# A gate projection moved from the attention heads into the product groups of the gate stage, with the first output projection as filler in its place

## The chip, the cores and the metric

The kernel runs on one core of a Trainium2 chip. The metric is the device time of one execution in microseconds (us); smaller is better. The engines named below are PE (TensorE, the matrix engine), DVE (VectorE), ACT (ScalarE), POOL (GpSimd) and SP (SyncE, which here only issues DMAs).

## The reference

One decoder block with two attention branches that read the same normalised input h (512 tokens, width 1024):

```python
proj = h @ w_in[layer]
fq, fk, fv, fz, mq, mk, mv, mz, ga, gb, fl = split_cols(proj, IN_SPLITS)
...
y_fox = from_heads(fox_attention(q, k, v, log_f)) * jax.nn.silu(fz)
...
y_moba = from_heads(moba_attention(q, k, v)) * jax.nn.silu(mz)
merged = (jax.nn.sigmoid(ga + b_gate[layer, 0]) * (y_fox @ w_fox[layer])
          + jax.nn.sigmoid(gb + b_gate[layer, 1]) * (y_moba @ w_moba[layer]))
x = x + merged @ w_out[layer]
```

Both branches have 8 heads of 64 columns, so q, k, v and z are 512 columns wide each; ga and gb have 1024 columns each. With 512 tokens the second branch sees at most its own block of 256 keys and the one before it, which together are all earlier keys: both branches are causal attention over 512 keys.

## The kernel before

**Numbers in two parts.** Every float32 operand of a large product is split into a high part in the matrix engine's reduced format and a low part, the rest. A product is then three matmuls (high by high, high by low, low by high). A split costs one ACT copy (`wh_...`, line 140) and one DVE subtraction (`wl_...`, line 142) for each 128x1024 block of weights. At most four split blocks exist at a time (tags `wh` and `wl`), and four raw blocks (`wr`), which SP loads in order as their buffers come free.

**Stages.** First come q and k of the first half of the first branch. Then follow the 16 heads, in four groups of four: first branch halves a and b (`f a`, `f b`), second branch halves a and b (`m a`, `m b`). After them stand the gates (`GA0`, `GA1` for ga, `GB0`, `GB1` for gb), the merge with the second output projection (`wm0` to `wm3`), and w_out.

**A head.** `Aa(h)` makes four tiles of logits (`lg`, 128, 256, 384 and 512 columns, two PSUM buffers); DVE takes the row maximum of each (line 574), ACT the exponential (576). `Bb(h)` transposes the tiles on PE (`p_a`, `p_b`, `p_cc`, three PSUM buffers of tag `tp`), ACT and DVE split them (`pth` 621, `ptl` 622), and PE multiplies by v (`pv`, 625 and 626; v is the stationary operand, tiles `v_mva`, `v_mvb`, tag `v`, two buffers). ACT and DVE then copy and add the two halves (`ysh` 650, `ypair` 651). `Tr` transposes q and k of a pair of heads (`p_qT`, `p_kT`, also tag `tp`), followed by ACT copies (538, 541, 543) and DVE remainders (539, 546). `sums_out` and `sums_in` send the inverse row sums through DRAM (`p_ri`, then the DMAs of lines 599 and 605, both on ACT's queue). `Yp` multiplies y by the inverse sums and by z (POOL 665, DVE 666) and splits it (667, 668).

**Fillers.** Between the steps of the heads stand units of projections that keep PE occupied: a list for each group of four heads, in `plan`. A q, k or v unit is 24 matmuls of 256 columns, a z unit (`unit_z`) 24 of 512 columns, a unit of the first output projection w_fox (`unit_f`, names wf0 to wf3, two units each) 12 of 512 columns. Filler results lie in two PSUM buffers (tag `pj`) until they are copied out; `unit_f` of wf0 copies into `f03`, a tile of tag `v`. The order in the program text is only the first order: the framework's scheduler then orders the instructions of all engines by its own estimates, and each engine works through its own list strictly in order.

**Groups of seven products.** Each of GA0, GA1, GB0 and GB1 makes two blocks of 256 columns by 512 tokens as seven products of half size in place of eight, in the manner of Strassen and Winograd: four on sums of the input halves (`S1` to `S4`, made in the first group of heads, kept in DRAM and loaded into SBUF by POOL's DMAs in `load_sums`) and three on the input itself (`A11`, `A12`, `A22`). One product is 24 matmuls of 256 columns. Four raw weight blocks (11, 12, 22, 21, loaded in this order) give seven weight operands (`prep`, with four subtractions on line 718). `PRODUCTS` sets the order of the products and `evac` what is kept or added after each.

## Time and profile before

| what | us |
|---|---|
| median of three runs | 424.02 |
| lowest and highest of them | 423.7, 426.01 |
| span of the profiled execution | 421.9 |
| PE busy in it | 416.7 |
| DVE busy | 326.8 |
| ACT busy | 280.4 |
| POOL busy | 101.7 |

The span runs from the first to the last instruction of the profiled execution; the 2.1 us between it and the median lie around it. PE is busy in 99% of the span, and the chain that ended last is 97% PE. So the kernel is read as a row of matmuls with hardly a hole, in which the other engines have to be on time. In the trace a matmul's duration overlaps that of its successor, so the price of one in a row is the distance between starts.

### The profile page before, as it was taken

The numbers are of one execution on the slowest core, as the hardware profiler recorded it, in microseconds if no ns is written. First come the engines' busy times: TensorE is split into PE (matmuls) and PEld (weight loads), VectorE is DVE, ScalarE is ACT, GpSimd is POOL, SyncE is SP. The second block draws the span as 40 slices with busy tenths as digits, with TensorE's granted clock in tenths as the row PEclk, the third lists the DMA queues.
The fourth block names the chain that finished last, engine by engine and source line by source line (L and its number), as shares of the span: only waits on it lengthen the run. The fifth ranks groups of instructions, "written<-read, shape, count | busy, mean of one in ns | idle before, by whom it ended". The sixth has DMA issues, their size and how long they took to land.

```text
span 421.9 us, 7677 instructions
## 1 busy us (share of the span) xinstructions
PE 416.7 (99%) x2909; PEld 387.6 (92%) x2909; DVE 326.8 (77%) x574; ACT 280.4 (66%) x529; POOL 101.7 (24%) x119
## 2 busy tenths in 40 slices
PE   8999999999999999999999999999999999999996
PEld 6998899999999998899998888899999989988885
DVE  4669968799968778568666779767979698689883
ACT  5987327877867978569758687655756535686450
POOL 1067600223236550015650101211000000022230
PEclk9999999999999999999999999999999999999999
DMA  7982335567153123303122310674052603697484
GB/s 237 391 285 99 99 101 162 154 195 223 59 172 103 42 87 101 97 29 99 36 92 76 101 50 27 233 248 143 26 177 64 236 2 112 220 248 119 100 136 164
DMA packets 24660, 56.37 MB, mean 134 GB/s; under 512 B 2864, under 2 KB 7664, under 8 KB 24624
## 3 DMA queue, kind: packets, MB, share of 16 engines
q1 hardware_dynamic: 13536, 38.11, 27.7%
q0 software_dynamic: 3392, 8.39, 8.8%
q10 hardware_dynamic: 7696, 9.38, 7.0%
q8 instruction: 23, 0.38, 0.4%
q14 instruction: 13, 0.11, 0.1%
HBM read 48.37 MB, written 6.32 MB: 130 GB/s over the span
## 4 chain that ended last, share of the span: by engine, by line
PE 97%; DMA 1%; SPq 0%; DVE 0%; issue 0%
PE pb_GB L757 3%; PE pb_GA L757 3%; PE pb_GB L754 3%; PE pb_GA L756 3%; PE pb_GB L756 3%; PE pb_GA L754 3%; PE po L945 3%; PE po L944 3%; PE po L943 3%; PE pv L626 2%; PE lg L572 2%; PE pv L625 2%; PE lg L571 2%; PE pf L684 2%; PE pf L683 2%; PE pf L685 2%
## 5 line engine op out<-in xcount | busy, mean ns | idle before, releaser
L342 POOL TENSOR_TENSOR ff<-ss,mh 128x8 f32<-128x8 f32 x16 | 29.7, 1861 | 73.2 <-DVE ss L340 67.4
L576 ACT ACTIVATE p<-p,negm 128x128 f32<-128x128 f32 (+1 forms) x64 | 35.7, 559 | 11.7 <-DVE negm L574 10.6
L574 DVE CUSTOM_DVE_ANT_0 p<-lg,mask 128x128 f32<-128x128 f32 (+1 forms) x64 | 30.8, 487 | 14.4 <-PE lg L572 13.9
L892 POOL DMA_DIRECT2D wr_o<-in_w_out_dram x4 | 4.9, 1279 | 89.3 <-DMA wr_o<-in_w_out_dram 81.1
L140 ACT ACTIVATE wh_GB<-wr_gb 128x1024 fp32r<-128x1024 f32 x14 | 14.6, 1059 | 10.1 <-PE pm L684 3.5
L571 PE MATMUL lg<-KH,QS 128*128 128x128 f32 (+1 forms) x64 | 20.4, 328 | 0.0
L906 DVE TENSOR_TENSOR wl_o<-wr_o,wh_o 128x1024 fp32r<-128x1024 f32 x14 | 17.0, 1222 | 3.8 <-ACT wh_o L905 3.8
L142 DVE TENSOR_TENSOR wl_GB<-wr_gb,wh_GB 128x1024 fp32r<-128x1024 f32 x14 | 16.9, 1223 | 3.9 <-ACT wh_GB L140 3.9
L905 ACT ACTIVATE wh_o<-wr_o 128x1024 fp32r<-128x1024 f32 x14 | 14.9, 1061 | 7.5 <-PE pb_GB L756 2.8
L142 DVE TENSOR_TENSOR wl_GA<-wr_ga,wh_GA 128x1024 fp32r<-128x1024 f32 x14 | 16.9, 1222 | 2.8 <-ACT wh_GA L140 2.3
L140 ACT ACTIVATE wh_GA<-wr_ga 128x1024 fp32r<-128x1024 f32 x14 | 14.6, 1057 | 5.9 <-PE pb_GA L756 2.7
L651 DVE TENSOR_TENSOR ypair<-pv,ysh 64x512 f32<-64x512 f32 x16 | 11.0, 687 | 6.6 <-ACT ysh L650 6.4
L622 DVE TENSOR_TENSOR ptl<-p_a,pth 128x512 fp32r<-128x512 f32 x16 | 11.0, 685 | 4.9 <-ACT pth L621 4.8
L650 ACT ACTIVATE ysh<-pv 64x512 f32<-64x512 f32 x16 | 9.5, 594 | 7.9 <-PE pv L626 5.5
L546 DVE SCALAR_TENSOR_TENSOR KL<-p_kT,cs,KH 64x512 fp32r<-64x512 f32 x16 | 12.0, 748 | 3.3 <-ACT KH L543 3.0
L336 DVE TENSOR_REDUCE ss<-sq 128x8 f32<-128x512 f32 x16 | 10.8, 680 | 4.3 <-ACT sq L335 4.2
L756 PE MATMUL pb_GA<-Gl,wh_GA 128*128 128x256 f32 x48 | 13.7, 285 | 0.0
L757 PE MATMUL pb_GA<-Gh,wl_GA 128*128 128x256 f32 x48 | 13.5, 281 | 0.0
L754 PE MATMUL pb_GA<-Gh,wh_GA 128*128 128x256 f32 x48 | 13.5, 280 | 0.0
L757 PE MATMUL pb_GB<-Gh,wl_GB 128*128 128x256 f32 x48 | 13.5, 281 | 0.0
L756 PE MATMUL pb_GB<-Gl,wh_GB 128*128 128x256 f32 x48 | 13.4, 281 | 0.0
L754 PE MATMUL pb_GB<-Gh,wh_GB 128*128 128x256 f32 x48 | 13.3, 281 | 0.0
(456 smaller groups left out, 1792.0 us busy)
## 6 DMA issues: line engine op xcount, KB each, us to landing
wr_ga<-in_w_in_dram SPq DMA_DIRECT2D x8, 512.0 KB
wr_gb<-in_w_in_dram SPq DMA_DIRECT2D x8, 512.0 KB
wr_o<-in_w_out_dram SPq DMA_DIRECT2D x8, 512.0 KB
xt<-in_xT_dram SPq DMA_DIRECT2D x8, 256.0 KB
x<-in_x_dram SPq DMA_DIRECT2D x8, 256.0 KB
s_dramh<-sum_sh ACTq DMA_DIRECT2D x8, 256.0 KB
s_draml<-sum_sl ACTq DMA_DIRECT2D x8, 256.0 KB
rinv_bc<-r_dram ACTq DMA_DIRECT2D x16, 128.0 KB
```

What stands on the lines that cost most here:

```text
L140: A.activation(hi[:, :, 0:n], src, AF.Copy)
L142: eng.tensor_tensor(out=lo[:, q, 0:n], in0=src[:, q], in1=hi[:, q, 0:n].bitcast(F32), op=OP.subtract)
L342: G.tensor_tensor(out=f2, in0=ss.rearrange("p t h -> p (t h)"), in1=mh, op=OP.pow)
L571: T.matmul(lg[:, :n], qs[:, qt], kh[:, :n], start=True, stop=False)
L574: V.tensor_tensor_reduce(pt, lg[:, :n], mask[:, 512 - n:512], -0.125, 3.0e38, op0=OP.add, op1=OP.min, accum_out=mkn[:, hh, i:i + 1])
L576: A.activation(pt, pt, AF.Exp, bias=mkn[:, hh, i:i + 1], scale=-1.0, accum_out=rs[:, hh, i:i + 1])
L754: T.matmul(o, hi[:, k, cc], lh, start=(n < 3 and c == 0 and k == 0), stop=False, skip_group_check=True)
L756: T.matmul(o, hi[:, k, cc], ll, start=False, stop=False, skip_group_check=True)
L757: T.matmul(o, lo[:, k, cc], lh, start=False, stop=(k == 3), skip_group_check=True)
L905: A.activation(wide(hi), wide(R[key, c]), AF.Copy)
L906: V.tensor_tensor(out=wide(lo), in0=wide(R[key, c]), in1=wide(hi).bitcast(F32), op=OP.subtract)
L943: T.matmul(o, gh, hi[:, c, r, :], start=(new and k == 0), stop=False, skip_group_check=True)
```

## The change

The second branch's z (mz, names mza and mzb) is no longer projected by four `unit_z` among the heads. It becomes a group of seven products like the gates, `GZ0`, ahead of GA0. Its results go through tanh and z in `finish_z`, and y of the second branch (kept as `YM`, without z) is multiplied by z there and split (`y_parts`). The filler lists move up: mqb goes to the group `f b`, the group `m a` has mkb and mvb, and the group `m b` has wf0 to wf3. The two wf3 units that stood behind the last head are gone from there. In all groups A12 changes place with S3, so the second product needs the raw block 21 and no sums.

```diff
--- before.py
+++ after.py
@@ -507,7 +507,15 @@
                 G.memset(tl[rows, :].bitcast(F32), 0.0)
 
 
-    Y = {}
+    Y, YM = {}, {}
+
+    def y_parts(br, gp, y):
+        yh = t2("y", 15, f"yh{br}{gp}", dt=F32R)
+        yl = t2("y", 15, f"yl{br}{gp}", dt=F32R)
+        A.activation(yh, y, AF.Copy)
+        V.tensor_tensor(out=yl, in0=y, in1=yh.bitcast(F32), op=OP.subtract)
+        Y[br, gp] = (yh, yl)
+
     mkn = con.tile([P, 16, 4], F32, name="negm")
     rs = con.tile([P, 16, 4], F32, name="rsum")
     ri = con.tile([P, 16, 4], F32, name="rinv")
@@ -659,14 +667,14 @@
             def go():
                 y = st["y", pr]
                 gp = 2 * (half == "b") + pr
-                yh = t2("y", 15, f"yh{br}{gp}", dt=F32R)
-                yl = t2("y", 15, f"yl{br}{gp}", dt=F32R)
                 zr = st["r", pr]
+                if not fox:
+                    ym = YM[gp] = t2("y", 15, f"ym{gp}")
+                    V.tensor_tensor(out=ym, in0=y, in1=zr, op=OP.mult)
+                    return
                 G.tensor_tensor(out=zr, in0=ZS[br, gp], in1=zr, op=OP.mult)
                 V.tensor_tensor(out=y, in0=y, in1=zr, op=OP.mult)
-                A.activation(yh, y, AF.Copy)
-                V.tensor_tensor(out=yl, in0=y, in1=yh.bitcast(F32), op=OP.subtract)
-                Y[br, gp] = (yh, yl)
+                y_parts(br, gp, y)
             return go
 
 
@@ -704,12 +712,12 @@
 
 
 
-    PRODUCTS = (("A11", 1), ("S3", 3), ("A12", 2), ("S2", 1), ("S1", 1), ("A22", 3), ("S4", 1))
+    PRODUCTS = (("A11", 1), ("A12", 2), ("S3", 3), ("S2", 1), ("S1", 1), ("A22", 3), ("S4", 1))
     groups = {}
 
     def group(name):
-        ga, i = name[1] == "A", int(name[2])
-        wa, wb = (f"g{'a' if ga else 'b'}{i}", f"g{'a' if ga else 'b'}{i + 2}")
+        ga, gz, i = name[1] == "A", name[1] == "Z", int(name[2])
+        wa, wb = ("mza", "mzb") if gz else (f"g{'a' if ga else 'b'}{i}", f"g{'a' if ga else 'b'}{i + 2}")
         st = {}
         R, B = {}, {}
         base = len(preps)
@@ -726,14 +734,14 @@
         def prep(n):
 
             def go():
-                if n == 1:
+                if n == 2:
                     sub(R["11"], R["12"], R["11"])
                     sub(R["12"], R["22"], R["12"])
                 elif n == 3:
                     sub(R["12"], R["22"], R["11"])
                 elif n == 5:
                     sub(R["21"], R["21"], R["12"])
-                key = ("11", "12", "21", "12", "11", "21", "22")[n]
+                key = ("11", "21", "12", "12", "11", "21", "22")[n]
                 B[n] = split(R[key], CW, f"{name}{n}")
             return go
         for key, nm, hf, last in (("11", wa, 0, 4), ("12", wb, 0, 5), ("22", wb, 1, 6), ("21", wa, 1, 5)):
@@ -775,9 +783,9 @@
                     u = [v4[:, 0:2, :], v4[:, 2:4, :]]
                 st["u"] = u
                 keep(1, 1)
+            elif n == 2:
+                keep(3, 3)
             elif n == 1:
-                keep(3, 3)
-            elif n == 2:
                 add(st["u"][0], 0, 1, 2)
             elif n == 3:
                 keep(2, 1)
@@ -789,7 +797,21 @@
             else:
                 finish(1)
 
+        def finish_z(q):
+            u = st["u"][q]
+            for c in range(2):
+                s = t2("u", 4, "sg")
+                for h in ((slice(0, S),) if q == 0 else (slice(0, HT), slice(HT, S))):
+                    z = two(st[1])[:, c, :] if q and h.start == 0 else u[:, c, h]
+                    A.activation(s[:, h], z, AF.Tanh, scale=0.5)
+                    V.scalar_tensor_tensor(u[:, c, h], s[:, h], 1.0, z, op0=OP.add, op1=OP.mult)
+                ym = YM[2 * q + c]
+                G.tensor_tensor(out=ym, in0=u[:, c, :], in1=ym, op=OP.mult)
+                y_parts("m", 2 * q + c, ym)
+
         def finish(q):
+            if gz:
+                return finish_z(q)
             u, j0 = st["u"][q], 2 * i + 4 * q
             bg = C_BG + (0 if ga else 8)
             for c in range(2):
@@ -989,8 +1011,8 @@
         groups["WO"] = late_loads
 
 
-    order = ["fqa", "fka", "fza", "fzb", "fva", "fqb", "fkb", "fvb", "mqa", "mka", "mva", "mza", "mqb", "mkb", "mvb", "mzb", "wf0", "wf1", "wf2", "wf3",
-             "GA0", "GA1", "GB0", "wm0", "wm2",
+    order = ["fqa", "fka", "fza", "fzb", "fva", "fqb", "fkb", "fvb", "mqa", "mka", "mva", "mqb", "mkb", "mvb", "wf0", "wf1", "wf2", "wf3",
+             "GZ0", "GA0", "GA1", "GB0", "wm0", "wm2",
              "GB1", "wm1", "wm3", "WO"]
     for nm in order[2:]:
         stream(nm)
@@ -1059,9 +1081,9 @@
     zero_kl()
     rope_tables()
     plan = (("f", "a", C_FQ, C_FK, ["fqb", "fkb", "fvb", "mqa"]),
-            ("f", "b", C_FQ, C_FK, ["mka", "mva", "mza"]),
-            ("m", "a", C_MQ, C_MK, ["mqb", "mkb", "mvb"]),
-            ("m", "b", C_MQ, C_MK, ["mzb", "wf0", "wf1", "wf2"]))
+            ("f", "b", C_FQ, C_FK, ["mka", "mva", "mqb"]),
+            ("m", "a", C_MQ, C_MK, ["mkb", "mvb"]),
+            ("m", "b", C_MQ, C_MK, ["wf0", "wf1", "wf2", "wf3"]))
     head, body, tail, gate = attn_group("f", "a", col(C_FQ), col(C_FK))
     head[0]()
     for n in range(4):
@@ -1094,10 +1116,9 @@
             at = 2
             body, tail = nxt[1][:at] + gate + nxt[1][at:], nxt[2]
             gate = nxt[3]
-    seq(["wf3"])
     enter("gates")
     load_sums()
-    fill = filler(["GA0", "GA1", "GB0"])
+    fill = filler(["GZ0", "GA0", "GA1", "GB0"])
     for n, u in enumerate(fill):
         u()
         if n == 2:
```

On PE, where the first units of wf0 stand among the last heads of `m a`, the kernel before has (pz_mzb is the second z unit of mzb, pf_3376 the first unit of wf0):

```order
L413 MATMUL pz_mzb_3329<-Gh,wh_mzb_3017 128x512
L571 MATMUL lg<-KH,QS 128x128
L572 MATMUL lg<-KL_852,QS 128x128
L414 MATMUL pz_mzb_3329<-Gl,wh_mzb_3017 128x512
L415 MATMUL pz_mzb_3329<-Gh,wl_mzb_3018 128x512
L683 MATMUL pf_3376<-yhf_1446,wh_wf_3263 128x512
L684 MATMUL pf_3376<-ylf_1447,wh_wf_3263 128x512
L625 MATMUL pv<-pth,v_mva 128x512
L626 MATMUL pv<-ptl,v_mva 128x512
```

Now the two units of wf0 (pf_3201 and pf_3241) stand earlier, and behind pf_3241 no filler follows until the first unit of wf1, pf_3261:

```order
L539 MATMUL p_kT<-ident,qn_mkb 128x128 x4
L634 MATMUL pv<-ptl,v_mva 128x256
L623 MATMUL p_a<-ident,p_3168 128x128
L623 MATMUL p_a<-ident,p_3174 128x128
L623 MATMUL p_a<-ident,p_3180 128x128
L623 MATMUL p_a<-ident,p_3186 128x128
L579 MATMUL lg<-KH,QS 128x128
L579 MATMUL lg<-KH,QS 128x256
L691 MATMUL pf_3261<-yhf_1448,wh_wf_2916 128x512
L692 MATMUL pf_3261<-ylf_1449,wh_wf_2916 128x512
```

From pf_3241 to pf_3261 there are 51 matmuls of the heads in a row; the last piece of them is shown.

On ACT, the copies of the filler results of wf0 stand in the kernel before as follows:

```order
L432 ACTIVATE sg<-pz_mzb_3329 128x512
L650 ACTIVATE ysh<-pv 64x512
L576 ACTIVATE p_3313,rsum<-p_3313,negm 128x256
L576 ACTIVATE p_3319,rsum<-p_3319,negm 128x384
L697 ACTIVATE f_3389<-pf_3376 128x512
L538 ACTIVATE QS<-p_qT,cs 64x512
L667 ACTIVATE yhm_3358<-ypair 128x512
```

Now the copies of both units of wf0 stand together behind the `ysh` of the last `m a` head:

```order
L549 ACTIVATE KH<-p_kT,cs 64x512
L551 ACTIVATE KH<-p_kT,cs 64x512
L658 ACTIVATE ysh<-pv 64x512
L705 ACTIVATE f_3214<-pf_3201 128x512
L705 ACTIVATE f_3214<-pf_3241 128x512
L629 ACTIVATE pth<-p_a 128x512
L584 ACTIVATE p_3231,rsum<-p_3231,negm 128x384
```

The target f_3214 is the tile f03 in the buffer of v_mva, so both copies come after the last matmul by v_mva.

On DVE, in that same stretch between two tiles of logits of neighbouring heads, there now stands preparation of GZ0 (wr_mza, wr_mzb), of which this is a piece:

```order
L726 TENSOR_TENSOR wr_mza_2914<-wr_mzb_2920,wr_mza_2914 128x1024
L630 TENSOR_TENSOR ptl<-p_a,pth 128x512
L582 ISA p_3219,negm<-lg,mask 128x128
L582 ISA negm 128x1
L659 TENSOR_TENSOR ypair<-pv,ysh 64x512
L582 ISA p_3225,negm<-lg,mask 128x256
```

The first row is one of GZ0's four subtractions of 1024 columns; in the kernel before no such subtraction stood on DVE before the third head of the last group.

## Rows read from the trace of the kernel before

**Rows 1.** The page, part 1: busy us, share of the span, instructions.

```profile
PE 416.7 (99%) x2909; PEld 387.6 (92%) x2909; DVE 326.8 (77%) x574; ACT 280.4 (66%) x529; POOL 101.7 (24%) x119
```

**Rows 2.** Stretches: length, busy by engine (instructions), PE clock, DMA share, GB/s.

```profile
226.30:280.00 53.70, 53.70 (x303) 46.35 (x302) 40.79 (x79) 39.87 (x85) 7.85 (x10) 1.00 0.35 116
282.00:310.00 28.00, 28.00 (x239) 28.00 (x238) 21.23 (x22) 16.84 (x24) 1.28 (x1) 1.00 0.43 139
```

**Rows 3.** PE in order of time, around the first wf0: start, us, line, tiles.

```profile
233.60 0.34 PE L572 MATMUL lg<-KL,QS 128*128 128x384 f32 x1
...
235.03 0.40 PE L413 MATMUL pz_mzb<-Gh,wh_mzb 128*128 128x512 f32 x1
...
238.54 0.40 PE L413 MATMUL pz_mzb<-Gh,wh_mzb 128*128 128x512 f32 x1
```

**Rows 4.** PE in order of time, a row of head matmuls without filler.

```profile
258.83 0.40 PE L571 MATMUL lg<-KH,QS 128*128 128x512 f32 x1
...
261.20 0.44 PE L684 MATMUL pf<-ylf,wh_wf 128*128 128x512 f32 x1
```

**Rows 5.** DVE groups by form: count, busy us, mean ns, idle before.

```profile
L539 DVE SCALAR_TENSOR_TENSOR QS<-p_qT,cs,QS 64x512 fp32r<-64x512 f32 x16 | 12.0, 750 | 1.2 <-ACT QS L538 0.8
L651 DVE TENSOR_TENSOR ypair<-pv,ysh 64x512 f32<-64x512 f32 x16 | 11.0, 687 | 6.6 <-ACT ysh L650 6.4
L574 DVE CUSTOM_DVE_ANT_0 p<-lg,mask 128x512 f32<-128x512 f32 x16 | 11.0, 686 | 3.9 <-PE lg L572 3.8
L622 DVE TENSOR_TENSOR ptl<-p_a,pth 128x512 fp32r<-128x512 f32 x16 | 11.0, 685 | 4.9 <-ACT pth L621 4.8
L718 DVE TENSOR_TENSOR wr_ga<-wr_ga,wr_ga 128x1024 f32<-128x1024 f32 x8 | 9.8, 1221 | 0.1
L574 DVE CUSTOM_DVE_ANT_0 p<-lg,mask 128x384 f32<-128x384 f32 x16 | 8.9, 554 | 4.0 <-PE lg L572 3.7
L574 DVE CUSTOM_DVE_ANT_0 p<-lg,mask 128x256 f32<-128x256 f32 x16 | 6.7, 418 | 4.0 <-PE lg L572 4.0
L574 DVE CUSTOM_DVE_ANT_0 p<-lg,mask 128x128 f32<-128x128 f32 x16 | 4.6, 288 | 2.5 <-PE lg L572 2.4
```

**Rows 6.** DVE in order of time: start, us, tiles, idle before and what ended it.

```profile
128.11 1.98 DVE L142 TENSOR_TENSOR wl_mva<-wr_mva,wh_mva 128x1024 fp32r<-128x1024 f32 x1
...
233.98 0.56 DVE L574 CUSTOM_DVE_ANT_0 p<-lg,mask 128x384 f32<-128x384 f32 x1 [0.42 <-PE lg L572]
...
288.50 0.69 DVE L666 TENSOR_TENSOR ypair<-ypair,rinv_bc 128x512 f32<-128x512 f32 x1 [3.08 <-POOL rinv_bc L665]
...
302.51 3.49 DVE L142 TENSOR_TENSOR wl_GA<-wr_ga,wh_GA 128x1024 fp32r<-128x1024 f32 x3
```

**Rows 7.** ACT groups by form: count, busy us, mean ns, idle before.

```profile
L140 ACT ACTIVATE wh_GA<-wr_ga 128x1024 fp32r<-128x1024 f32 x14 | 14.6, 1057 | 5.9 <-PE pb_GA L756 2.7 <-PE pf L684 1.5 <-issue 1.3
L541 ACT ACTIVATE KH<-p_kT,cs 64x512 fp32r<-64x512 f32 x16 | 10.9, 679 | 1.2 <-PE p_kT L531 1.0
L650 ACT ACTIVATE ysh<-pv 64x512 f32<-64x512 f32 x16 | 9.5, 594 | 7.9 <-PE pv L626 5.5 <-PE p_b L615 2.2
L697 ACT ACTIVATE f<-pf 128x512 f32<-128x512 f32 x8 | 4.6, 590 | 0.6 <-PE pf L685 0.5
```

**Rows 8.** ACT's queue in order of time: inverse sums to DRAM, and back.

```profile
230.86 0.27 ACTq L599 DMA_DIRECT2D r_dram<-rinv_t  x1
...
233.75 1.11 ACTq L605 DMA_DIRECT2D rinv_bc<-r_dram  x2
```

**Rows 9.** PE in order of time: the last transpose of inverse sums.

```profile
275.56 0.27 PE L596 MATMUL p_ri<-ident,rinv 128*8 128x128 f32 x1
```

**Rows 10.** DMA issues: count, KB each, us to landing.

```profile
S0h<-s_dramh POOLq DMA_DIRECT2D x1, 512.0 KB, 4.1
```

**Rows 11.** POOL in order of time: a product of z beside splits on DVE.

```profile
126.98 2.03 POOL L665 TENSOR_TENSOR rinv_bc<-zs_fza,rinv_bc 128x512 f32<-128x512 f32 x1 [1.49 <-DMA rinv_bc<-r_dram]
```

**Rows 12.** PE in order of time: the first matmuls of the kernel.

```profile
1.12 3.93 PE L104 MATMUL warm_ps<-warm 128*128 128x512 f32 x9 [1.12 <-DVE fg_pre L479]
```

## The prediction

> **What bounds the kernel now.** First comes part 1 of the page, the busy time of each engine [rows 1]: PE is busy for 416.7 us of a span of 421.9, 99%, and DVE, the next, 77%. Then the table by stretches [rows 2], since a share over the whole span hides stages: in the heads of the second branch (226.30 to 280.00) PE is busy for 53.70 of 53.70 us, in a stretch of GA0 and GA1 for 28.00 of 28.00, both at a granted clock of 1.00. So a matmul that is saved is time saved, but only while the other engines are on time. DVE has 12.9 us to spare in the first stretch and 6.8 in the second; that is an average, and the change alters who waits for whom within it.
>
> **What the z projection saves.** The price of a matmul in a row is the distance between starts. In the stretch of gate products 239 of 256 columns take 28.00 us, 0.117 each [rows 2]. From 235.03 to 238.54 lie 15 matmuls of 512 columns, 0.234 each [rows 3]. Out go four z units of 24: 96 × 0.234 = 22.5 us. In come seven products of 24: 168 × 0.117 = 19.7. That is one eighth less, −2.8; I take −2.6, since a group also begins with PSUM buffers to be handed over. Moving mqb, mkb, mvb and wf as such costs nothing: they remain on PE one for one, under PE work.
>
> **A stretch without fillers.** Fillers also cover the softmax of the heads, and this is where I expect the gain to be lost. In the kernel before, two units of mzb were the first fillers of the group `m b`; they end a few matmuls behind the 15 counted above [rows 3], and only then came wf0, when v_mva was almost done with. Now wf0's two units come first. Both PSUM buffers of tag `pj` then hold wf0, whose copies go into f03. That tile is the buffer of v_mva, so both copies wait for the last `pv` of the last `m a` head, and the ACT list has them behind that head's `ysh`. Until then no filler can start, and PE's list has 51 head matmuls in a row. Before, the longest such row that I read is 19, from 258.83 to 261.20, 2.37 us or 0.125 each [rows 4]. So 51 are 6.4 us of work, and the 48 of them behind the 384-column logits of the first `m b` head are 6.0.
>
> Who has to work in those 6.0 us? In PE's row stand tiles of logits of the first `m b` heads, and there are two `lg` buffers: each tile waits until DVE has read the one two places earlier. The tile of 256 that opens the next head stands directly ahead of wf1. Between the 384-column tile and that point DVE's list has 14 operations. By their rows [rows 5]: row maxima 0.55 + 0.69 + 0.29 + 0.42 + 0.55 + 0.69 = 3.19; remainders of transposed tiles 0.69 + 0.69, and 0.42 for a tile of 256 (an estimate, from the row maximum of that width), together 1.79; `ypair` 0.69; `QS` 0.75; two of GZ0's subtractions of 1024 columns, 1.22 each, 2.44; and its first split remainder, 1.22 alone. These are 10.07. In a row they overlap a little: three remainders take 3.49 [rows 6], 1.16 each, some 0.06 to 0.09 less per step, so I take 1.1 off and have 9.0. DVE starts on a tile 0.38 after its last matmul began (233.60 on PE [rows 3], 233.98 on DVE [rows 6]): 9.4. ACT's way ends a little later: behind DVE's work come two `KH` (0.68 each), `ysh` (0.59) and the copies of wf0 (0.59 each) [rows 7], and they let wf1 start at about 9.7. Against 6.0 us of matmuls PE waits 3.7.
>
> Two bounds on that. `p_cc` of the first head needs one of three `tp` buffers, held by `p_kT` until DVE has made the remainder from it behind a split of wf3: 0 to 1.1, I take 0.6. On ACT the pair of heads' DMAs lie ahead of these copies; in the trace the second one's issue comes 2.9 us after the first (230.86 to 233.75), with 1.11 for the two issues [rows 8]. If that falls into the stretch, ACT is later by up to 1.1 more than I count; if GZ0's three DVE pieces (3.5 us together) find idle time before the stretch, almost all of the wait goes. I take 3.7 + 0.6 = 4.3, with ends of 0.2 and 5.5. A gain is excluded here: the matmuls of the stretch stay as many, and before PE had no idle time in it to give back [rows 2].
>
> **The hand-over to the gates.** The preparation of GZ0's seventh product (S4) has on DVE ahead of it the product of y and the inverse sums, which waits for the sums' way through DRAM. Before, the last `p_ri` is at 275.56 [rows 9] and DVE multiplies at 288.50 after an idle 3.08 [rows 6]: 12.9, of which POOL's product of z (1.28 [rows 2]) now drops out, 11.7. Only when S4 is split does a raw buffer come free for GA0's block 21, and by the new order GA0's second product, A12, needs it. The chain goes on with the multiplication 0.69 and DVE's split 1.16 to 1.22 [rows 6], the load (an estimate: 512 KB landed 4.1 after issue [rows 10]), ACT's copy 1.06 [rows 7] and DVE's split 1.2: 11.7 + 8.2 = 19.9, or 21.2 if POOL's product was no part of the way. PE's work over the same time: six of GZ0's products, 144 × 0.117 = 16.9, and some 24 head matmuls × 0.125 = 3.0, together 19.9, up to 20.4. It is a near thing: I take 0.4, with ends of 0 and 3.1, the idle time that this wait showed. With S3 in second place, as before, one more product (2.8 us) would lie in between.
>
> GZ0 also brings four products by z on POOL, 1.28 each [rows 2], beside DVE's splits. Before, a split remainder that began at 128.11 took 1.98 in place of 1.16 [rows 6] while such a product was at work, and the product took 2.03 (126.98 to 129.01) [rows 11]: 0.75 to 0.82 more for each. In the new lists the first two of them come behind the split for A12, so they delay later operands, which have up to four products of lead: 0 in the sum, up to 1.6 for two. The Trainium skill has a rule that speaks against the change here ("SBUF — State Buffer", "Who interferes with whom"): a VectorE instruction with two SBUF inputs and a GpSimd instruction that reads SBUF can't run together, and the later one is blocked to the end of the earlier. The trace agrees, as the 1.98 shows; by the full block, twice 1.28, the sum would be up to 2.6 higher, by the row 1.6.
>
> The rest costs nothing: the new order of the products doesn't change the number of matmuls, tanh and the sums of `finish_z` lie under 168 matmuls (ACT has 11 us to spare in 28 [rows 2]), and the wf3 units at the end only change place.
>
> **The sum.** 421.9 − 2.6 + 4.3 + 0.4 = 424.0 for the span. The median of before, 424.02, is 2.1 above its profiled span, so the time is 426.1.
>
> **Rivals.**
>
> Half cover: the gaps in the heads are partly filled because DVE, with time to spare up to there, does GZ0's pieces earlier; half of the 4.3 remain, 2.1. Span 421.8, time 423.9; 423 to 425.
>
> Full cover: DVE and ACT catch up, both bounds at their low ends: 421.9 − 2.6 + 0.2 to 0.6, and 0 to 0.5 at the gates; time 421.4 to 422.7, around 422. For it: 12.9 us of idle DVE in the stretch. Against it: the order on each engine is fixed, and the wait is a chain of single steps, not of sums.
>
> The gates' chain ends late: the inverse sums through DRAM, then block 21, then A12. If the heads hold DVE and ACT up, the chain is late by the full 3.1 and PE waits 2.3 to 2.7 more than I count: 428.4 to 428.8, slower than before. It decides once the way from `p_ri` to GA0's second product takes more than 20.4 us.
>
> POOL shuts DVE out: two of GZ0's products by z each stretch a DVE split by 0.75 to 0.82, at a point where DVE has no lead; 426.1 + 1.6 = 427.7, slower. For it is the one collision read above; against it the lead of the operands. It is the rule named there, taken by the row's price.
>
> The clock falls: in the kernel's first nine matmuls of 512 columns PE took 3.93 us, 0.437 each [rows 12], against 0.234 later, so it ran at half pace, 1.2 of 2.4 GHz, after idling. If the gaps in the filler-less stretch brought that about, its 6.0 us of matmuls would take 12.0 where 9.7 were needed, 2.3 more: 428.4. Against it: a granted clock of 1.00 in both stretches [rows 2], and gaps of a fraction of a us each. The Trainium skill says that PE goes back to half rate when it is idle ("TensorE: Matmul & The Clock Gate", Part 1); no row of the kernel before shows that in its middle.
>
> **How the numbers follow.** About 0.5% is what a measurement of this kernel can tell from no change: under 421.9 is faster, over 426.1 slower. My forecast has 0.52, with a range of its own of 425.0 to 427.3, half of it on each side of the bound (0.26 same, 0.26 slower). Half cover has 0.08 (same), full cover 0.15 (0.10 faster, 0.05 same), the gates' chain 0.15, POOL 0.05 and the clock 0.05 (all slower). Together: faster 0.10, same 0.39, slower 0.51. The range from 422.5 to 428.5 leaves out most of full cover and the upper ends of the late cases, about 2 in 10 together.
>
> **What the profile after would show.** The saving: GZ0's 168 matmuls in some 19.7 us, PE's busy time 2.6 to 2.8 lower apart from gaps. The stretch: between pf of wf0 and pf of wf1, PE idle for 3 to 5 us in all, ended by DVE at logits and by ACT at wf1's first matmul; full cover would show less than 1. The gates: DVE's idle time for the inverse sums before S4's split, then PE waiting for GA0's second operand by 0 to 1; if by 2 or more, the chain rival is right. The clock: below 1.00 anywhere in the heads would confirm that rival. The forecast is wrong if PE's row stays closed behind wf0, or if PE waits elsewhere for something that I took as covered.

## The result and the profile after

The changed kernel takes 429.57 us (median of four runs, 429.24 to 430.95) against 423.94 for the kernel before (four runs, 423.7 to 426.01): a ratio, estimated from all the executions, of 1.0119, with a 95% interval of 1.0073 to 1.0166. It is slower, to which the prediction gave 0.51, but by 5.6 us where 2.1 were forecast, and it lies above the range given. The profiled execution has a span of 427.7 against 421.9.

The page's part 1 of the changed kernel (busy us, share of the span, instructions), beside [rows 1]:

```profile
PE 417.4 (98%) x2981; PEld 390.1 (91%) x2981; DVE 339.1 (79%) x586; ACT 284.4 (66%) x537; POOL 105.8 (25%) x119
```

PE's busy time hardly tells anything here: it is 0.7 higher than before, although its matmuls need less time. The profile models the ends of matmuls, and part of each gap counts as busy in it: of the first gap below, 1.40 us by starts, 1.24 are shown as idle. The chain of part 4 tells more. Before, it was 97% PE; now 12% of it lies on other engines and DMAs:

```profile
PE 88%; DVE 5%; DMA 3%; ACT 2%; issue 1%; SPq 0%; DVEq 0%; ACTq 0%
```

**Where the time went.** For each matmul I took the distance to the next start and subtracted the usual distance of its shape (0.061, 0.118, 0.176 and 0.233 us for 128, 256, 384 and 512 columns in both kernels; 0.085 for a transpose, which is a mean, since the single distances are 0.11 or 0.03). What remains is time that PE lost. By these distances the saved matmuls bring 96 × 0.233 − 168 × 0.118 = 2.5 us. The losses, as the difference from the kernel before:

| stretch (us) | what runs there | lost more than before |
|---|---|---|
| 215 to 245 | end of `m a`, first heads of `m b` | 4.2 |
| 245 to 272 | last heads, start of GZ0 | 0.7 |
| 272 to 330 | end of GZ0, GA0, GA1 | 2.9 |
| all others | start, first branch, end | 0.6 |

421.9 − 2.5 + 4.2 + 0.7 + 2.9 + 0.6 = 427.8; the span is 427.7.

**Among the heads.** PE in order of time behind wf0 (start, us, tiles, idle before and what ended it). The first row is a transpose of q, the next two are logits, the last is the first matmul of wf1:

```profile
224.94 0.44 PE L537 MATMUL p_qT<-ident,qn_mqb 128*128 128x128 f32 x2 [1.24 <-DVE ptl L630]
...
229.54 0.33 PE L579 MATMUL lg<-KH,QS 128*128 128x128 f32 x1 [0.91 <-ACT KH L551]
230.13 0.39 PE L579 MATMUL lg<-KH,QS 128*128 128x256 f32 x1 [0.27 <-DVE negm L582]
230.64 0.50 PE L691 MATMUL pf<-yhf,wh_wf 128*128 128x512 f32 x1
```

These are nearly the places that the prediction named: a `tp` buffer (it had the wait at `p_cc`, not at `p_qT`), the logits' buffers, `KH`, and in the end wf1. Counted by starts, the four gaps are 1.40, 1.09, 0.53 and 0.39, which is 3.4 of the 4.2. The table of that stretch (length, then busy us and instructions of PE, PEld, DVE, ACT and POOL, granted clock, DMA share, GB/s), to be held against PE's 53.70 of 53.70 in [rows 2]:

```profile
219.90:230.70 10.80, 8.24 (x54) 6.80 (x52) 9.80 (x21) 8.92 (x20) 0.55 (x1) 1.00 0.24 84
```

DVE is busy for 9.80 of 10.80 and ACT for 8.92: with no filler in PE's row, both others are nearly full.

**At the gates.** The first row below is the last transpose of inverse sums. In the second, GZ0's second product waits, 0.6 us by starts, for its PSUM bank, which the transposes of the last head hold:

```profile
258.80 0.27 PE L604 MATMUL p_ri<-ident,rinv 128*8 128x128 f32 x1
...
261.21 0.39 PE L762 MATMUL pb_GZ<-Gh,wh_GZ 128*128 128x256 f32 x1 [0.41 <-DVE ptl L630]
```

DVE, at the end of GZ0, answers to the third row of [rows 6]:

```profile
271.87 0.69 DVE L673 TENSOR_TENSOR ym<-ypair,rinv_bc 128x512 f32<-128x512 f32 x1 [3.69 <-DMA rinv_bc<-r_dram]
272.48 1.22 DVE L142 TENSOR_TENSOR wl_GZ<-wr_mzb,wh_GZ 128x1024 fp32r<-128x1024 f32 x1
```

The last `p_ri` is at 258.80, so the inverse sums took 13.1 us to come back. Not all of that is the way through DRAM: on ACT's queue 6.1 us lie between the issue to DRAM and the issue back, which comes only when ACT, after waiting 2.57 us for a matmul of GZ0, has gone on in its list. No run moved that issue, so what it is worth is not shown. ACT and its queue:

```profile
259.55 0.27 ACTq L607 DMA_DIRECT2D r_dram<-rinv_t  x1
...
264.24 1.06 ACT L140 ACTIVATE wh_GZ<-wr_mza 128x1024 fp32r<-128x1024 f32 x1 [2.57 <-PE pb_GZ L764]
...
265.63 1.10 ACTq L613 DMA_DIRECT2D rinv_bc<-r_dram  x2
```

S4's split is done at 273.7 (272.48 + 1.22). Then block 21 is loaded, and PE waits three times, here with what ended the wait:

```profile
280.58 0.39 PE L762 MATMUL pb_GA<-S0h,wh_GA 128*128 128x256 f32 x1 [0.50 <-ACT wh_GA L140]
...
292.87 0.39 PE L765 MATMUL pb_GA<-Gh,wl_GA 128*128 128x256 f32 x1 [0.43 <-DVE wl_GA L142]
...
296.77 0.38 PE L762 MATMUL pb_GA<-Gh,wh_GA 128*128 128x256 f32 x1 [1.03 <-ACT wh_GA L140]
```

By starts these are 0.66, 0.59 and 1.19, at GA0's third product (S3), at its A22 and at GA1's first. ACT at the same places: it waits 4.7 us for block 21, and its copy for the third product comes behind that block's copy and two tanh. Later it stands 3.4 us in front of a copy of y that needs POOL's product by z, with the next weight operand behind it in its list:

```profile
277.48 1.06 ACT L140 ACTIVATE wh_GA<-wr_ga 128x1024 fp32r<-128x1024 f32 x1 [4.71 <-DMA wr_ga<-in_w_in_dram]
278.44 1.14 ACT L806 ACTIVATE sg<-uGZ 128x512 f32<-128x512 f32 x2
279.49 1.04 ACT L140 ACTIVATE wh_GA<-wr_ga 128x1024 fp32r<-128x1024 f32 x1
...
295.14 0.63 ACT L515 ACTIVATE yhm<-ym 128x512 fp32r<-128x512 f32 x1 [3.38 <-POOL ym L809]
295.68 1.04 ACT L140 ACTIVATE wh_GA<-wr_ga 128x1024 fp32r<-128x1024 f32 x1
```

The table of this stretch in the kernel before and, in the second row, in the changed one (same columns as above); DVE's 27.62 of 38.00 us have become 35.63:

```profile
272.00:310.00 38.00, 38.00 (x312) 37.50 (x311) 27.62 (x31) 23.47 (x34) 2.90 (x4) 1.00 0.51 170
272.00:310.00 38.00, 36.04 (x295) 35.02 (x294) 35.63 (x38) 23.40 (x35) 8.83 (x4) 1.00 0.22 71
```

### The profile page after: what moved, and what is told of

It reads as the page before. It is cut to its first block, busy times and chain, and to the rows that moved or that the text cites. A ratio compares the mean times of both kernels' runs of the same rounds, so it can differ in the third digit from the quotient of the medians.

```text
span 427.7 us, 7845 instructions
## 1 busy us (share of the span) xinstructions
PE 417.4 (98%) x2981; PEld 390.1 (91%) x2981; DVE 339.1 (79%) x586; ACT 284.4 (66%) x537; POOL 105.8 (25%) x119
## 4 chain that ended last, share of the span: by engine, by line
PE 88%; DVE 5%; DMA 3%; ACT 2%; issue 1%; SPq 0%; DVEq 0%; ACTq 0%
PE pb_GB L765 3%; PE pb_GB L762 3%; PE pb_GB L764 3%; PE po L967 3%; PE po L966 3%; PE po L965 3%; PE pb_GA L762 2%; PE pb_GA L765 2%; PE lg L580 2%; PE pv L633 2%; PE pb_GA L764 2%; PE lg L579 2%; PE pv L634 2%; PE pf L691 2%; PE pm L692 2%; PE pm L691 2%
## 5 line engine op out<-in xcount | busy, mean ns | idle before, releaser
L584 ACT ACTIVATE p<-p,negm 128x128 f32<-128x128 f32 (+1 forms) x64 | 35.8, 561 | 13.1 <-DVE negm L582 11.9
L579 PE MATMUL lg<-KH,QS 128*128 128x128 f32 (+1 forms) x64 | 21.3, 341 | 1.2 <-ACT KH L551 0.9
L659 DVE TENSOR_TENSOR ypair<-pv,ysh 64x512 f32<-64x512 f32 x16 | 11.0, 687 | 10.1 <-ACT ysh L658 9.8
L809 POOL TENSOR_TENSOR ym<-uGZ,ym 128x512 f32<-128x512 f32 x4 | 8.8, 2225 | 22.2 <-DVE uGZ L807 22.2
L579 PEld LDWEIGHTS lg<-KH,QS 128*128 128x128 f32 x64 | 12.1, 189 | 2.2 <-ACT KH L551 1.1
```

Source lines behind the costliest of these rows:

```text
L579: T.matmul(lg[:, :n], qs[:, qt], kh[:, :n], start=True, stop=False)
L584: A.activation(pt, pt, AF.Exp, bias=mkn[:, hh, i:i + 1], scale=-1.0, accum_out=rs[:, hh, i:i + 1])
```

## The experiments

Each is a change to the changed kernel, but for the first. The times of the kernel before beside them were 423.88 to 424.10 in the medians. "Lost" is time lost on PE in one profiled execution, by the measure above, more than in the kernel before.

| label | lost 215–245 | 245–272 | 272–330 | median us | ratio to before, 95% |
|---|---|---|---|---|---|
| the changed kernel | 4.2 | 0.7 | 2.9 | 429.57 | 1.0073 to 1.0166 |
| e1_swap_only | 0.0 | 0.1 | 5.7 | 430.06 | 1.0109 to 1.0166 |
| e2_no_swap | 5.5 | 1.7 | 2.7 | 430.71 | 1.0109 to 1.0174 |
| e3_wf_results_apart | 0.1 | 3.9 | 1.0 | 427.49 | 1.0046 to 1.0107 |
| e4_gz_later | 4.1 | 0.3 | 4.3 | 432.00 | 1.0137 to 1.0221 |
| e5_z_on_dve | 4.2 | 0.7 | 3.2 | 430.24 | 1.0118 to 1.0185 |
| e6_sums_later | 4.1 | 0.8 | 3.6 | 430.06 | 1.0111 to 1.0153 |
| e7_f_banks | 0.1 | 1.5 | 5.0 | 428.16 | 1.0076 to 1.0110 |
| e8_f_banks_sums | 0.1 | 1.5 | 4.0 | 426.91 | 1.0041 to 1.0085 |
| e9_load_order | 5.6 | 0.9 | 3.5 | 429.87 | 1.0071 to 1.0167 |
| e10_f_banks_sums_loads | 0.1 | 1.5 | −0.1 | 423.42 | 0.9958 to 1.0001 |
| e11_parts_later | 0.1 | 1.5 | 3.7 | 426.83 | 1.0030 to 1.0077 |
| e12_sums_loads | 4.1 | 0.8 | 0.0 | 428.11 | 1.0075 to 1.0113 |

Some of the losses hold a short spell at half clock (the last section): about 1.5 us each in the first column of e2 and e9 and in the third of e1, e6 and e8. The medians come from four executions or more, of which the columns show one.

### e1_swap_only: the order of products alone

The edit is on the kernel before; `prep` and `evac` change with it as in the change itself.

```diff
-    PRODUCTS = (("A11", 1), ("S3", 3), ("A12", 2), ("S2", 1), ("S1", 1), ("A22", 3), ("S4", 1))
+    PRODUCTS = (("A11", 1), ("A12", 2), ("S3", 3), ("S2", 1), ("S1", 1), ("A22", 3), ("S4", 1))
```

> The kernel before with one part of the change alone: A12 ahead of S3 in all groups; mz stays among the heads. Theory (the loss comes from the heads and from GZ0's hand-over, not from the order of products): 423.5 to 425, and PE's waits in the gate stage as in the kernel before, under 1 us in all. Rival (the new order itself costs, since the raw block 21 is needed earlier): 425.5 to 427, with PE waiting at the second product of GA1 or GB0.

430.06: the theory falls, and the rival had another place and less time. One wait of 4 us makes the loss, in GA0, with a spell at half clock behind it. ACT in the kernel before (first fence), then ACT and PE of this run (start, us, tiles, idle before):

```profile
286.79 0.58 ACT L764 ACTIVATE e_GA<-pb_GA 128x512 f32<-128x512 f32 x1
289.23 0.63 ACT L667 ACTIVATE yhm<-ypair 128x512 fp32r<-128x512 f32 x1 [1.86 <-DVE ypair L666]
```

```profile
291.73 0.63 ACT L667 ACTIVATE yhm<-ypair 128x512 fp32r<-128x512 f32 x1 [4.68 <-DVE ypair L666]
292.27 0.58 ACT L764 ACTIVATE e_GA<-pb_GA 128x512 f32<-128x512 f32 x1
```

```profile
292.90 0.39 PE L754 MATMUL pb_GA<-Gh,wh_GA 128*128 128x256 f32 x1 [3.98 <-ACT e_GA L764]
```

The copy of y for the last pair of heads waits for the inverse sums, and with the new order it came to stand in ACT's list ahead of the copy that empties a PSUM bank of GA0; before, that copy stood in front. So on the kernel before the order of products alone brings a loss, by way of ACT's list: what stands behind the wait for the inverse sums in a strict list is late.

### e2_no_swap: the change without the new order

```diff
-    PRODUCTS = (("A11", 1), ("A12", 2), ("S3", 3), ("S2", 1), ("S1", 1), ("A22", 3), ("S4", 1))
+    PRODUCTS = (("A11", 1), ("S3", 3), ("A12", 2), ("S2", 1), ("S1", 1), ("A22", 3), ("S4", 1))
```

> The changed kernel with the old order of products (S3 second, A12 third); all else as changed. Theory (block 21 of GA0 comes too late because its buffer is freed behind the wait for the inverse sums, and the swap needs it one product earlier): the waits at the start of GA0 shrink by 0.5 to 1.5 us, 428 to 429; the heads keep their wait of about 4 us. Rival (the waits in GA0 come from ACT and POOL, whatever the order): 429 to 430.

430.71, and 2.7 us lost at the gates against 2.9. The theory falls: with GZ0 in place there is a late operand in both orders. Another 1.4 us is lost at a `pv` among the last heads. The heads' larger loss is the same four gaps (1.40, 1.10, 0.53, 0.39) and a spell at half clock behind them.

### e3_wf_results_apart: results of wf0 and wf1 in tiles of their own

```diff
-            if j == 0:
-                f = sb.tile([P, 4, S], F32, name="f03", tag="v", bufs=2)
-                FS[0], FS[1] = f[:, 0:2, :], f[:, 2:4, :]
-            elif j in (4, 6):
+            if c == 0:
                 FS[j // 2] = sb.tile([P, 2, S], F32, name=f"f{j}", tag="qk", bufs=4)
...
-                if ga or i == 0:
-                    u = [sb.tile([P, 2, S], F32, name=f"u{name}{q}", tag="qk", bufs=4) for q in range(2)]
-                else:
+                if True:
                     v4 = sb.tile([P, 4, S], F32, name=f"u{name}", tag="v", bufs=2)
```

> The changed kernel with one cause taken away: the results of wf0 and wf1 go into two tiles of the q and k buffers, which are free by then, and all groups of seven put their results into the v buffers. So wf0's copies no longer wait for the last matmul by v_mva. Theory (the filler-less row of 51 head matmuls costs 4 us): the wait at the first heads of the last group falls from 4 us to under 1 and the time to 425 to 426.5. Rival (heads without cover cost the same wherever they stand: here a row of 44 head matmuls stands between products of GZ0): the wait moves there, 427.5 to 429.5.

Both are half right. The 4.2 us at wf0 are gone, so the buffer of v_mva was the cause there. But 3.9 were lost among the last heads, where PE's list now had 44 head matmuls between two products of GZ0. PE in that row:

```profile
256.73 0.50 PE L633 MATMUL pv<-pth,v_mvb 128*128 128x512 f32 x1 [1.93 <-DVE ypair L659]
...
260.25 0.49 PE L633 MATMUL pv<-pth,v_mvb 128*128 128x512 f32 x1 [0.56 <-ACT pth L629]
```

The table of that row shows that here neither engine is full (DVE 7.79 and ACT 6.65 of 10.00 us): PE waits for the steps of a head one after the other.

```profile
252.00:262.00 10.00, 7.28 (x46) 5.93 (x45) 7.79 (x16) 6.65 (x16) 3.20 (x6) 1.00 0.73 249
```

427.49, 2.1 less than the changed kernel.

### e4_gz_later: GZ0's operands later

```diff
-        preps.extend(prep(n) for n in range(7))
+        def later(go):
+            def pinned():
+                with behind():
+                    go()
+            return pinned
+        preps.extend(later(prep(n)) if gz and n < 3 else prep(n) for n in range(7))
```

`behind()` queues what is in it on DVE behind the instruction that was written last for DVE.

> The changed kernel with DVE's work for GZ0's first three weight operands queued behind the heads' maxima, out of the filler-less row, which itself stays (57 head matmuls). Theory (the wait there is DVE's chain, of which these pieces are 3.5 us): the wait falls from 4 us to 0.5 to 1.5; the operands are later, which may cost up to 2 at the start of GZ0: 426 to 428.5. Rival (ACT's copies of wf0 behind the last head end the wait whatever DVE does): 3.5 to 4 us of wait remain, 429 to 430.

432.00, above both numbers, with 4.3 us lost at the gates. PE lost 4.1 us in the stretch, as if nothing had been taken from DVE. The table of the same stretch of this run shows why:

```profile
219.90:230.70 10.80, 9.02 (x56) 6.94 (x55) 7.88 (x21) 10.32 (x25) 0.55 (x1) 1.00 0.24 82
```

DVE went from 9.80 to 7.88, and ACT from 8.92 to 10.32 of 10.80. A row of heads without fillers fills ACT almost as soon as DVE. The size in the prediction was right (3.7 for that chain), but the loss stays without DVE's pieces for GZ0. The test is not clean: the row has 57 head matmuls here, not 51, and ACT's instructions stand in another order.

### e5_z_on_dve: products by z on DVE

```diff
-                G.tensor_tensor(out=ym, in0=u[:, c, :], in1=ym, op=OP.mult)
+                V.tensor_tensor(out=ym, in0=u[:, c, :], in1=ym, op=OP.mult)
```

> The changed kernel with the four products by z on DVE in place of POOL. In the changed kernel they took 2.2 us each on POOL beside DVE's work, and ACT stood 5.0 us in all waiting for them, with its copy of the next weight operand behind. Theory (these waits of ACT cause PE's wait of 1.2 us at the first product of GA1): ACT no longer waits there, PE's waits between 290 and 300 fall from 1.8 to under 0.8: 428 to 429. Rival (DVE, which gets 2.4 us more to do, is what is late there): the waits stay or grow, 429.5 to 431.

430.24. ACT's waits for POOL are gone, and so is PE's wait of 1.2 at GA1's first product; but 1.4 came at GA1's fourth instead, ended by DVE, and GA0's third waits 1.1 in place of 0.7. The rival is right: the stage's losses stay at 3.2.

```profile
311.51 0.39 PE L765 MATMUL pb_GA<-S1h,wl_GA 128*128 128x256 f32 x1 [1.21 <-DVE wl_GA L142]
```

### e6_sums_later: the last inverse sums behind S4

```diff
-        if n == 2:
+        if n == 5:
             gate[0]()
```

> The changed kernel with the multiplication of the last pair of heads by its inverse sums moved behind GZ0's sixth product, so that on DVE it stands behind the split of S4, which no longer waits for DRAM. Theory (DVE's idle 3.7 us there starts the backlog that PE meets at GA0's third, fifth and GA1's first operand): these three waits, 2.4 us in all, fall under 0.8 and the time to 427 to 428; the heads keep their 4 us. Rival (the backlog comes from the products by z and their splits, whenever block 21 is loaded): at most the first wait of 0.7 goes, 428.5 to 429.5.

430.06, so neither number. The three waits went, and one of 2.6 came, at GA1's third product, with a spell at half clock. ACT had waited for a block of GA1 that SP had loaded late, and the third operand's copy followed behind it:

```profile
298.16 1.07 ACT L140 ACTIVATE wh_GA<-wr_ga 128x1024 fp32r<-128x1024 f32 x1 [1.40 <-DMA wr_ga<-in_w_in_dram]
```

The loss moved back by one group.

### e7_f_banks: other PSUM banks for GZ0

With the edit of the third experiment:

```diff
-                st[b] = pst(("pj", "tp", "tp")[b - 1], (2, 3, 3)[b - 1], f"pb{b}_{name}")
+                st[b] = (pst(("pj", "lg", "lg")[b - 1], 2, f"pb{b}_{name}") if gz else
+                         pst(("pj", "tp", "tp")[b - 1], (2, 3, 3)[b - 1], f"pb{b}_{name}"))
```

> The third experiment (results of wf0 and wf1 in tiles of their own) with GZ0's second and third PSUM bank taken from the two banks of the logits, which are free earlier than those of the transposes. So a whole product of GZ0 stands between the last two heads and the row of 44 head matmuls becomes rows of 22 and 27. Theory (uncovered rows cost, by the length of the row): the 3.9 us that the third experiment lost among the last heads fall under 1.5, and the time to 424 to 425.5. Rival (the last heads are bound by their own chain through ACT and DVE): 426.5 to 427.5.

Among the last heads the loss fell from 3.9 to 1.5 as the theory has it. The time did not fall (428.16, above both numbers): PE came to GA0 earlier, and lost 5.0 in GA0 and at GA1's start to the same late operands.

### e8_f_banks_sums: banks and inverse sums together

The edits of the sixth and the seventh in one.

> The same with the last multiplication by the inverse sums behind the split of S4 as well. Theory: what is left in GA0 and GA1 (1.4 us in the third experiment) falls under 0.5: 423 to 424.5. Rival: no difference to the run before.

426.91, 1.3 under the run before, so neither theory nor rival. One wait is left in the gate stage, and it is the one that the sixth experiment ended with:

```profile
299.34 0.39 PE L760 MATMUL pb_GA<-S0h,wh_GA 128*128 128x256 f32 x1 [2.54 <-ACT wh_GA L140]
```

ACT ahead of it (the last row is GA1's second operand, from block 21):

```profile
292.48 0.63 ACT L515 ACTIVATE yhm<-ym 128x512 fp32r<-128x512 f32 x1 [1.60 <-POOL ym L805]
294.62 1.06 ACT L140 ACTIVATE wh_GA<-wr_ga 128x1024 fp32r<-128x1024 f32 x1 [1.51 <-DMA wr_ga<-in_w_in_dram]
```

The third operand follows at 298.24, behind the load of a table and two sigmoids, and PE waits for it. Block 21 is the last of the four that SP loads, and the new order of products uses it second.

### e9_load_order: the raw blocks in the order of use

```diff
-        for key, nm, hf, last in (("11", wa, 0, 4), ("12", wb, 0, 5), ("22", wb, 1, 6), ("21", wa, 1, 5)):
+        for key, nm, hf, last in (("11", wa, 0, 4), ("21", wa, 1, 5), ("12", wb, 0, 5), ("22", wb, 1, 6)):
```

> The changed kernel with the raw blocks loaded in the order in which its products need them: 11, 21, 12, 22 in place of 11, 12, 22, 21. So block 21 no longer waits for the buffer that the split of S4 frees, which stands behind the wait for the inverse sums. Theory (the late block 21 is the cause of PE's waits in GA0 and of the backlog that makes GA1's): these waits, 2.4 us in all, fall under 1: 427.5 to 428.5; the heads keep 4 us. Rival (the backlog is ACT's and DVE's, behind POOL's products by z): 429 to 430.

429.87, the rival's number, and 3.5 us lost at the gates, no less than before the edit: 0.8 at GA0's third product, 0.9, 0.6 and 1.2 at three operands behind it. Alone it does nothing: the third product then waits for block 22, whose buffer S4's split frees, still behind the inverse sums. DVE's second subtraction for it waits for that block:

```profile
280.17 1.23 DVE L726 TENSOR_TENSOR wr_ga<-wr_ga,wr_ga 128x1024 f32<-128x1024 f32 x1 [1.39 <-DMA wr_ga<-in_w_in_dram]
```

### e10_f_banks_sums_loads: all of these together

The edits of the third, sixth, seventh and ninth experiments.

> The eighth experiment (results of wf0 and wf1 apart, banks of the logits, last inverse sums behind S4) with the load order 11, 21, 12, 22. Theory of late blocks: the wait of 2.7 us in GA1 goes, 424 to 425. Rival (ACT's copies behind POOL's products by z): 426 to 427 as before.

423.42 us (ten runs, 422.34 to 424.79), a little under the theory's numbers, against 424.03: a ratio of 0.998 with an interval of 0.9958 to 1.0001. The gate stage lost nothing more than before. All that is left of PE's waits in this run, besides the start of the kernel:

```profile
PE pv L633 <- DVE ypair L659: 0.3, 1, 0.3
```

So 2.5 us of saved matmuls minus 1.5 that the last heads still lose: about 1 us (the span of the profiled execution is 420.6), and by the medians 0.6, which the interval doesn't clear. The gate stage has hardly room left for more on DVE; its table, DVE 37.00 of 38.00 us (27.62 in the kernel before):

```profile
272.00:310.00 38.00, 38.00 (x319) 37.81 (x318) 37.00 (x39) 24.80 (x36) 9.84 (x4) 1.00 0.29 92
```

### e11_parts_later: the splits of y queued later

On the run above; `late_parts` calls `y_parts` with its ACT and DVE instructions queued behind the last ones written, at four later units of the gate stage.

```diff
-                y_parts("m", 2 * q + c, ym)
+                LATE.append((2 * q + c, ym))
...
+        if n == 11:
+            late_parts(1)
+        if n in (13, 15, 17):
+            late_parts(1)
```

> The run before it with the splits of the second branch's y (ACT's copies and DVE's remainders, which wait for POOL) queued behind work of GA0 and GA1, since they are needed only in the merge. Theory (with heads covered, blocks in time and ACT not waiting for POOL, the saved matmuls show): waits in the gate stage under 1 us, 422.5 to 424, at or just under the kernel before. Rival (ACT and DVE have too little time left in the stage): 425 to 427.

426.83, the rival's number. The run before lost nothing in the gate stage; this one lost 3.7, of which 1.6 came at GA0's third operand and 1.6 later. That DVE, already full, is the reason is argued, not shown.

### e12_sums_loads: the gates' two repairs alone

The edits of the sixth and ninth in one, on the changed kernel; the heads stay.

> The changed kernel with the two repairs of the gate stage alone (last multiplication by the inverse sums behind the split of S4, raw blocks in the order of use); the heads stay as changed, with the row of 51 head matmuls. Theory (two separate losses, about 4 us among the heads and about 3 at the gates, and the gates' needs both repairs at once): the waits in GA0 and GA1 go and the time is 426 to 427.3, the heads' 4 us remain. Rival (the gates came into order in the tenth experiment only because the heads ended earlier there): waits of 2 us or more in GA0 or GA1 and 428.5 to 430.

In the profiled execution, 426.44 us, the gate stage lost nothing and the heads 4.1, as the theory says. PE's waits in it:

```profile
PE p_qT L537 <- DVE ptl L630: 1.2, 1, 1.2
...
PE lg L579 <- ACT KH L551: 0.9, 1, 0.9
...
PE pb_GZ L762 <- DVE ptl L630: 0.4, 1, 0.4
PE lg L579 <- DVE negm L582: 0.3, 1, 0.3
```

The median, 428.11, is higher than forecast because in three of six executions PE's mean granted clock was 0.995 or 0.996 and the time 428.6 to 429.0. In the other three it was 0.998 to 1.00 and 426.4 to 427.6, against 429.2 to 429.7 for the changed kernel at 0.999 to 1.00.

## Why the prediction was wrong

**The saving** was nearly right: 2.8 forecast for the matmuls, 2.5 by the distances between starts. The price of 0.117 was read from 239 matmuls in 28.00 us, of which 236 start in that time, 0.119 each. The 0.2 taken off for PSUM buffers that change hands was too little: the start of GZ0 lost 0.7.

**The stretch without fillers** was right in place and size, 4.3 forecast and 4.2 lost, and only partly right in cause. That both `pj` buffers wait for v_mva's buffer is shown: e3 took that away, and the loss there went. That DVE's extra pieces for GZ0, 3.7 of the 10.1 us summed for DVE, are needed for the wait is not borne out: in e4 they are gone, ACT is nearly as full, and 4.1 are lost. So the right size is in part luck. What holds PE up is the softmax work of the heads on two engines, and e3 shows that it costs nearly as much at another place where no filler stands, there by its order of steps, with time left on both engines.

**The hand-over** is the step that failed: a term of 0.4 that measured 2.9, with 0.7 at the start of GZ0 in place of the 0.2. The working followed one chain, from the inverse sums to the second product of GA0, and that product indeed did not wait. Its high part was there at 278.5 and its low part at 279.80; its first matmul, on the high part, started at 279.68:

```profile
279.68 0.28 PE L762 MATMUL pb_GA<-Gh,wh_GA 128*128 128x256 f32 x1
```

```profile
276.61 1.22 DVE L726 TENSOR_TENSOR wr_ga<-wr_ga,wr_ga 128x1024 f32<-128x1024 f32 x1
278.57 1.23 DVE L142 TENSOR_TENSOR wl_GA<-wr_ga,wh_GA 128x1024 fp32r<-128x1024 f32 x1 [0.74 <-ACT wh_GA L140]
```

(The chain was 13.1 us to DVE, not 11.7; it was no shorter without POOL's product, so the 21.2 for the whole chain was the better value.) But the text stopped there. Behind the chain stood three more things. The third product needs DVE's two subtractions, the second of them the first row above, and an ACT copy; the subtractions stand behind the inverse sums in DVE's list, and the copy stands in ACT's behind that of the late block 21. DVE, idle for 3.7 us and then nearly full (35.63 of 38.00 us), had little room to catch up. And ACT's list had the copies of y behind POOL, ahead of GA1's first operand. The prediction looked at POOL's products with 0 in the sum and up to 1.6 beside it, and set the rest at "nothing" with ACT's 11 us to spare from [rows 2], an average over a stretch without GZ0's work. Three experiments took one thing away each, and the loss stayed: without ACT's wait for POOL (e5) and without DVE's wait for the sums (e6) it came back up to a group later, and with another load order (e9) it stayed about where it was. e12 took the wait and the load order away at once, and all 2.9 were gone. So the cause shown is the pair: S4's split behind the inverse sums, and raw blocks loaded in an order that no longer fits the products. Neither POOL's products by z nor DVE's full list is enough alone: in e12 the products take no less time (3.90 and 5.92 us for two each), and DVE is busy for 37.33 of the same 38.00 us, without a wait of PE. Whether the old order of products with the sums moved would have done as well was not tried.

The 0.7 at the start of GZ0: its second product needs a bank of tag `tp`, which the heads' transposes hold; it waited 0.6 at 261.2. The working had no wait for this bank beyond the 0.2; e7's other banks did away with a row of 44 but left 1.5.

**The rivals.** The one that came nearest is "the gates' chain ends late", with 428.4 to 428.8 and a chance of 0.15; the mechanism is right to half, since the chain took 21.0 us, more than the 20.4 of its condition, but the waits were not at A12 but behind it. Half and full cover did not come: none of the 4.3 was filled. The range was too narrow by its own terms: the two upper ends together, 5.5 and 3.1, would have given 430.0, and even the likely 4.3 with 3.1 at the gates gives 428.8, above the 428.5 that I set. (Full cover's own terms add up to 421.6 to 422.5, not 421.4 to 422.7.) POOL beside DVE was priced at 0 to 1.6; the four products took 2.2 us each in place of 1.28, and three of DVE's instructions beside them were stretched: a weight split to 1.72, a sum of z (0.40 alone) to 1.51 and a remainder of y (0.68 alone) to 1.08. e5 shows that taking the products off POOL doesn't help the time.

## What to carry to other kernels

A filler that is moved away from heads must be replaced where the cover is needed, and a filler whose result waits for a buffer of those same heads covers nothing: look at what each filler's result needs before it can leave PSUM. Where a wait is found on a hand-over, follow not only the first operand behind it but everything in the same strict lists, for two or three products, and set that against the busy share of this stage, not of its neighbours. When an order of use changes, look at the order of loads with it; here one repair of two left the loss or moved it on, and only both removed it.

## What the runs showed of the hardware

The granted clock fell in the middle of the kernel, which I had given 0.05. In e9's profiled execution PE was busy for 1.70 of 3.00 us among the uncovered heads, where no gap of the row was longer than 1.4 by starts; from about 232 to 235.6 it then ran at half pace, 1.2 GHz, while it was fully busy (stretches of 1 us show 0.58, 0.50, 0.50 and 0.71), and after that at 2.4 again. The table of three stretches:

```profile
228.00:231.00 3.00, 1.70 (x12) 1.12 (x10) 2.94 (x7) 2.50 (x5) 0.33 (x1) 1.00 0.53 175
233.00:235.00 2.00, 2.00 (x6) 1.51 (x6) 1.21 (x3) 1.94 (x5) 0.00 (x0) 0.50 0.00 0
237.00:240.00 3.00, 3.00 (x19) 2.53 (x18) 0.67 (x3) 1.33 (x2) 0.00 (x0) 1.00 0.02 5
```

It cost about 1.5 us there, and the executions of e12 with the lower mean clock took about 2 more. The same gaps in the changed kernel's profiled execution were followed by no fall. Over all executions, the mean granted clock was 0.996 or lower in 13 of 30 of the kernels that keep this row (the changed one, e2, e4, e5, e6, e9 and e12), in 2 of the 47 of the kernel before that were taken beside the experiments, and in none of e10's ten: the waits make the time uncertain as well as longer, though which wait brought a fall is shown only for the profiled executions. In e1 the fall followed the one wait of 4 us, in e8 that of 2.7; in e6 it began towards the end of the one of 2.6.

POOL and DVE hinder each other, in one case more than the 2.03 of [rows 11] let expect: the products by z of 128 x 512 took 1.28 alone and in the changed kernel, two in a row, 1.95 and 2.46 on average beside DVE's work, the longest 3.69:

```profile
280.48 3.91 POOL L809 TENSOR_TENSOR ym<-uGZ,ym 128x512 f32<-128x512 f32 x2 [15.21 <-DVE uGZ L807]
291.42 4.92 POOL L809 TENSOR_TENSOR ym<-uGZ,ym 128x512 f32<-128x512 f32 x2 [7.03 <-DVE uGZ L807]
```
